# A hybrid decoder step: part tiles for split weights, down blocks behind the value tile, norms a turn earlier

## The chip, the cores and the metric

The kernel runs on one core of a Trainium2 chip. The metric is the device time of one execution in microseconds (us), less is better. TensorE (PE) does the matmuls into PSUM banks, ScalarE (ACT), VectorE (DVE) and GpSimd (POOL) do the elementwise work, and SyncE (SP) issues the DMAs. Each engine works through its instructions in the order in which they stand in its own list, and waits for others at semaphores.

## The reference

One layer of a decoder in float32, for a prompt of 2048 rows (with 16 meta rows ahead) and 8 samples of 4 rows: a mixer (an RG-LRU and a Mamba-2 part beside each other), and then a convolutional feed-forward part:

```python
def conv_ffn(h, buf, w_up, cw, cb, w_down):
    u = h @ w_up                                      # 1024 -> 2 x 3072
    u, new_buf = causal_dwconv(u, buf, cw, cb)        # 3 taps along the rows
    g, v = u[..., :D_FF], u[..., D_FF:]
    return (jax.nn.gelu(g) * v) @ w_down, new_buf     # 3072 -> 1024

def trunk(x, ...):
    ...
    h = rmsnorm(x, p['norm_mix'][l])
    m, lc, lh, sc, ss = mixer(h, ...)
    x = x + m
    h = rmsnorm(x, p['norm_ffn'][l])
    f, fc = conv_ffn(h, st_ffn_conv[l], ...)
    x = x + f
    ...
    y = rmsnorm(x, p['norm_final'])
```

Outputs are `y` for both groups of rows and the states of the scans and convolutions.

## The kernel before

**Split products.** Every float32 matrix is split into a hi part in a format that TensorE takes whole (ACT, L109) and a lo part, raw less hi (DVE, L110). A product is three matmuls: hi by hi, hi by lo, lo by hi. A weight tile has 128 x 1024 elements. It is loaded into `wraw` (or `x`, `wraw2`), and `Plain.split` writes both parts into one tile `whl`, of which there are three.

**The program list.** The phases fill a list `prog` of steps, each with the weight tiles that it uses. `build` walks through the list. Before a step it issues the loads of the tiles of the next steps (`LOADS_B` tiles ahead in the later super tiles, `AHEAD` = 2 ahead before) and then the splits that come due. The order on PE is the order of the list; on ACT, DVE and POOL a scheduler orders what the steps issue, and each queue is then served in that order.

**The mixer** takes the rows in six turns (`PLAN_A`) and ends near 960 us. It keeps its result `x` in DRAM scratch.

**The ConvFFN** takes the rows in four super tiles. The first one (S0) has the 32 sample rows and 512 rows of the prompt. For each of the 24 channel tiles kk it multiplies a gate tile (`whole_g`, PSUM bank `mm`, 48 matmuls) and a value tile (`whole_v`, bank `yy`, 48 matmuls). `conv` copies the bank into `u` (ACT, L1017 to L1020) and makes the three taps (L1101 on ACT, two times L1103 on DVE); `join` multiplies gate and value into `pm` (samples, L1042) and `p` (L1044), and splits `p` into `ph`. For the later super tiles S0 also makes four sums and differences of the half tiles of each weight pair (`Sums.add`, POOL, L955 to L958), splits them into parts `ws` (`part`), and writes the parts to DRAM scratch `wk` (`keep`).

After four channel tiles there is a block of down products in two halves (512 columns of `w_down` each), one at each of the next two kk: `m` (L1145, eight matmuls of the samples with the raw weights), then the row tiles q0 to q3 with 12 matmuls each, in two `sg` banks in turn. DVE adds each bank to `acc` (m: L1152, q: L1122). The last block stands at the end of a super tile; the sample rows are summed at L1159 and L1160. `store` normalizes and writes the result (L1138).

Later super tiles (256 + 256 columns) read the parts back and need seven products of 12 matmuls for each kk (`first_part`, `second_part`, `third_part`).

**The next super tile's rows.** `norm(q)` loads a row tile of `x`, sums its squares (ACT, L152), makes `rstd` (POOL) and multiplies (DVE, L218). `turn(p, stage)` transposes it on PE (L228) and makes the seven `h` operands on ACT, DVE and POOL (L243 to L265); stages 0 to 3 for the pair p = 0 and for the pair p = 1. `norm` of rows 0 to 2 stands at kk = 22 (after the loop in S0), `norm(3)` and the turns stand among the last down products as a `side` dictionary of positions:

```python
for z in range(4):
    side[z].append(turns[z])
    side[len(rest) - 5 + z].append(turns[4 + z])
side[3].append(lambda n=n: n.norm(3))
```

Of the kernel before, what the change touches and what calls it, by code (L numbers as in the profile page):

```python
# [17 lines left out]
P = 128  # L18
# [16 lines left out]
START = len(PLAN_A[0])  # L35
START2 = 3 * START + 1
GT_BUFS = 2
LOADS_B, SPLITS_B = 3, 3


SLOTS = {
# [32 lines left out]
def build(tc, i, o):  # L74
# [5 lines left out]
    with contextlib.ExitStack() as es:  # L80
# [31 lines left out]
        class Plain:  # L112
# [7 lines left out]
                ld(self.raw, self.src)  # L120

            def split(self, E=V):
                hl = wp.tile([P, 2, 1024], F32R, name="whl", tag="whl")
                divide(hl[:, 0], hl[:, 1], self.raw, E)
                self.out = hl[:, 0], hl[:, 1], self.raw

        def mms(ps, pairs):
            for k, (l, r) in enumerate(pairs):
# [75 lines left out]
        class Halves:  # L204
# [7 lines left out]

            def norm(self, q):
                rows, load = self.tiles[q]
                x = self.x[q] = row_tile()
                y = load(x)
                r = rstd_of(sum_squares(y[:rows], rows, D), rows, D)
                V.scalar_tensor_tensor(x[:rows], y[:rows], r[:rows], gain[:rows], op0=MUL, op1=MUL)  # L218
# [78 lines left out]
        for n, (fn, srcs) in enumerate(prog):  # L297
            if n < START:
                fn()
                continue  # L300
            if n == START2:
                begin.close()
            bound = len(flat) if n > k.begin_b else early
            b = n > k.begin_c
            while loaded < min(bound, used + len(srcs) + (LOADS_B if b else AHEAD)):
                flat[loaded].load()
                loaded += 1
            while split < min(bound, used + len(srcs) + (SPLITS_B if b else AHEAD if n >= START2 else 0)):
                flat[split].split(*(() if split else (G,)))
                split += 1  # L310
            ws = [z.out for z in flat[used:used + len(srcs)]]
            used += len(srcs)
            if fn is k.tail:
                end = es.enter_context(tc.manual_schedule(engines=order))
                continue
            fn(*ws)
# [564 lines left out]
def phase_b(k, h_b):  # L881
# [7 lines left out]
    def setup():  # L889
        k.phase.close()  # L890
        cb = k.phase.enter_context(k.tc.tile_pool(name="cb", bufs=1))
        E.sp = k.phase.enter_context(k.tc.tile_pool(name="sb", bufs=2))
        for nm, shp in (("fcw", [P, 48, 3]), ("fcb", [P, 48]), ("sel4", [P, SROWS])):
            c[nm] = cb.tile(shp, F32, name=nm, tag=nm)
            ld(c[nm], i[nm])
        c["o_fc"] = cb.tile([P, 48, 9, 2], F32, name="o_fc", tag="o_fc")
        ld(c["o_fc"][:, :, 0:NS, :], i["st_fc"])
        turn = itertools.count()
        k.raws.append(lambda: tmp("cu"[next(turn) % 2], UW, CB)[:, :512])
        k.junks.append(lambda: tmp("c", UW, CB).bitcast(BF16))  # L900

    CB, PARTS = 3, 7
# [41 lines left out]
    class Sums:  # L944


        def __init__(self, kk):
            room = {} if not kk else {"room": k.row_tile}
            self.kk = kk
            self.g = k.Plain(i["w_up"][kk], **room)  # L950
            self.v = k.Plain(i["w_up"][24 + kk], **({"room": lambda: tmp("wraw2", D, 2)} if kk else {}))

# [8 lines left out]
        def part(self, z):  # L961
            hl = E_tile("ws", 512, PARTS)
            k.divide(hl[:, 0], hl[:, 1], self.raw[z])
            if z:
                self.keep(z - 1)
            self.hl = hl

        def keep(self, z):
            ld(kept[self.kk][z], self.hl.bitcast(F32))

    S = []
    for si in range(len(PLAN_B)):
# [209 lines left out]
    def first_super_tile(t):  # L1182
        ps = [Sums(kk) for kk in range(24)]
        for kk in range(24):
            add(whole_g(t, kk), ps[kk].g)
            if kk:
                for z in range(2):
                    add(lambda z=z, p=ps[kk - 1]: p.part(z))
            if kk == 2:
                add(lambda: accs(t))  # L1190
            for b in range(NBLK - 1):
                for half in range(2):
                    if kk == NB * (b + 1) + half:
                        for fn, srcs in downs(t, b, half):
                            add(fn, *srcs)
            add(whole_v(t, kk), ps[kk].v)
            if kk:
                for z in range(2, 4):
                    add(lambda z=z, p=ps[kk - 1]: p.part(z))
            if kk:  # L1200
                add(lambda p=ps[kk - 1]: p.keep(3))
            add(ps[kk].add)

        def end():
            k.side.close()
# [1 line left out]
        add(end)  # L1207
        for z in range(4):
            add(lambda z=z: ps[23].part(z))
        add(lambda: ps[23].keep(3))  # L1210

    def later_super_tile(t):
        for kk in range(24):
# [9 lines left out]
                for fn, srcs in downs(t, *z):  # L1223
                    add(fn, *srcs)
            if kk == 22 and t is not S[-1]:
                for q in range(3):
                    add(lambda q=q: S[t.si + 1].norm.norm(q))
            add(second_part(t, kk), Value(kk), *[Kept(kk, z) for z in range(4)])

    for t in S:  # L1230
# [2 lines left out]
        (first_super_tile if t.first else later_super_tile)(t)  # L1233
        if t.first:
            k.begin_c = len(k.prog)
            for q in range(3):
                add(lambda q=q, n=n: n.norm(q))
        else:
            add(third_part(t, 23))
# [4 lines left out]
        if not last:  # L1244
            turns = [lambda p=p, s=s, n=n: n.turn(p, s) for p in range(2) for s in range(4)]
            side = {z: [] for z in range(len(rest))}
            for z in range(4):
                side[z].append(turns[z])
                side[len(rest) - 5 + z].append(turns[4 + z])
            side[3].append(lambda n=n: n.norm(3))  # L1250
        nd = len(rest) - len(rest) // (2 if t.first else 3)
        for n, (fn, srcs) in enumerate(rest):
            if n == nd:
# [113 lines left out]
```

## Time and profile before

| | |
|---|---|
| median of three runs | 2635.69 us (2634.97 to 2640.7) |
| profiled execution | 2637.97 us, span 2635.8 us, mean granted TensorE clock 0.976 |
| mixer | 0 to 960 us |
| first super tile S0 | 960 to 1476 us |
| S1, S2, S3 | to 1862, 2250 and 2636 us |
| busy: PE, DVE, ACT, POOL | 94%, 74%, 46%, 26% of the span |

Times in the profile's timelines are us from the start of the span. "Idle before" is the time in which an engine stood still ahead of an instruction, with the instruction that ended it. The names are the program's: `mm`, `yy`, `tr` and `sg` are PSUM banks, `whl` a split weight tile, `ws` a part, `h` the operands of a super tile.

### The profile page before, as it was taken

What the parts mean: (1) busy time and instruction counts of PE and PEld (TensorE: products, weight loads), DVE (VectorE), ACT (ScalarE), POOL (GpSimd) and SP (SyncE); (2) the same over time, 40 slices, a digit from 0 to 9 for tenths busy, and PEclk for the clock granted to TensorE, in tenths of its full rate; (3) what the DMA queues carried; (4) which work ended last, traced back from release to release, by engine and by line L of the source; (5) the groups of instructions that cost most, each with busy time, mean ns of one, the idle gap of its engine ahead of it and who ended that gap; (6) DMA issues with size and microseconds to landing.
All of it is one profiled execution on the core that took longest, in us unless ns stands there. A gap on an engine that the chain in (4) does not pass through costs nothing.

```text
span 2635.8 us, 42301 instructions
## 1 busy us (share of the span) xinstructions
PE 2480.6 (94%) x15834; PEld 2248.0 (85%) x15834; DVE 1948.6 (74%) x3028; ACT 1215.3 (46%) x2005; POOL 673.6 (26%) x1059
## 2 busy tenths in 40 slices
PE   7899999999989898999998999999999999999998
PEld 6578888888878787887787799998899998999997
DVE  7588878789787876666666777777777777877675
ACT  5354645456464664444445443334443334433333
POOL 4332313233232434433334300002200002200001
PEclk9899999999999999999999999999999999999999
DMA  5344252432525376454445776665776665866563
GB/s 175 105 134 134 72 177 74 155 123 79 172 81 176 101 230 239 176 207 172 164 178 215 273 264 218 234 225 192 252 252 231 218 223 179 279 238 220 208 210 129
DMA packets 153801, 486.40 MB, mean 185 GB/s; under 512 B 23334, under 2 KB 23718, under 8 KB 153596
## 3 DMA queue, kind: packets, MB, share of 16 engines
q1 hardware_dynamic: 153596, 483.70, 53.7%
q8 instruction: 125, 2.05, 0.3%
q14 instruction: 80, 0.66, 0.1%
HBM read 413.27 MB, written 70.37 MB: 183 GB/s over the span
## 4 chain that ended last, share of the span: by engine, by line
PE 67%; DVE 15%; issue 7%; POOL 4%; ACT 4%; DMA 3%; SPq 0%; DVEq 0%; POOLq 0%; ACTq 0%
PE mm L129 25%; PE sg L129 15%; PE yy L129 12%; PE tr L129 8%; DVE whl L110 3%; DVE cv L496 3%; ACT whl L109 1%; POOL wraw L956 1%; POOL wraw L955 1%; DVE acc L1122 1%; DMA wraw<-in_w_down 1%; POOL x L957 1%; PE yy L678 1%; DVE xbc L592 1%; DVE ws L110 1%
## 5 line engine op out<-in xcount | busy, mean ns | idle before, releaser
L129 PE MATMUL mm<-hhi,whl 128*128 128x384 f32 (+4 forms) x2688 | 637.9, 321 | 10.8 <-ACT xr L491 8.2
L110 DVE TENSOR_TENSOR whl<-wraw,whl 128x1024 fp32r<-128x1024 f32 x360 | 451.9, 1256 | 196.1 <-ACT whl L109 195.3
L129 PE MATMUL sg<-whl,ph 128*128 128x512 f32 x2304 | 554.6, 398 | 23.4 <-DVE acc L1122 22.8
L129 PEld LDWEIGHTS sg<-whl,ph 128*128 128x128 f32 x2304 | 431.7, 190 | 131.8 <-DVE acc L1122 30.8
L109 ACT ACTIVATE whl<-wraw 128x1024 fp32r<-128x1024 f32 x361 | 380.8, 1056 | 260.5 <-PE sg L129 105.8
L129 PEld LDWEIGHTS mm<-hhi,whl 128*128 128x128 f32 x2688 | 471.1, 193 | 17.2 <-ACT xr L491 9.9
L129 PE MATMUL mm<-hlo,whl 128*128 128x384 f32 (+4 forms) x1344 | 426.8, 318 | 0.9 <-DVE hlo L202 0.9
L1103 DVE SCALAR_TENSOR_TENSOR c<-u,fcw,c 128x512 f32<-128x512 f32 (+1 forms) x384 | 297.6, 805 | 24.6 <-ACT c L1101 20.5
L1099 POOL COPY o_fc<-u 128x2 f32<-128x2 f32 x192 | 55.5, 289 | 839.6 <-DVE u L1008 725.8
L129 PEld LDWEIGHTS mm<-hlo,whl 128*128 128x128 f32 x1344 | 259.6, 193 | 2.9 <-DVE hlo L202 1.2
L1101 ACT ACTIVATE c<-u,fcb,fcw 128x512 f32<-128x512 f32 (+1 forms) x192 | 154.0, 820 | 101.2 <-DVE u L1008 100.8
L129 PE MATMUL yy<-h,ws 128*128 128x256 f32 x1476 | 197.0, 283 | 0.0
L129 PE MATMUL tr<-h,ws 128*128 128x256 f32 x1440 | 191.9, 283 | 0.0
L129 PE MATMUL mm<-h,ws 128*128 128x256 f32 x1404 | 186.4, 282 | 4.9 <-DVE s L1069 4.9
L129 PEld LDWEIGHTS yy<-h,ws 128*128 128x128 f32 x1476 | 186.6, 190 | 1.0
L129 PEld LDWEIGHTS tr<-h,ws 128*128 128x128 f32 x1440 | 181.2, 190 | 0.7
L129 PEld LDWEIGHTS mm<-h,ws 128*128 128x128 f32 x1404 | 175.7, 189 | 5.7 <-DVE s L1069 5.3
L129 PE MATMUL mm<-whl,yhi 128*128 128x512 f32 (+1 forms) x544 | 174.7, 401 | 3.5 <-DVE whl L110 2.6
L1122 DVE TENSOR_TENSOR acc<-acc,sg 128x512 f32<-128x512 f32 x192 | 130.8, 682 | 61.3 <-PE sg L129 61.1
L129 PE MATMUL yy<-hhi,whl 128*128 128x274 f32 (+1 forms) x768 | 152.7, 292 | 4.7 <-ACT u L1020 4.7
L496 DVE SCALAR_TENSOR_TENSOR cv<-xr,packed,cv 128x384 f32<-128x384 f32 (+2 forms) x216 | 146.8, 682 | 3.4 <-ACT cv L494 0.3
L129 PEld LDWEIGHTS yy<-hhi,whl 128*128 128x128 f32 x768 | 124.8, 192 | 5.6 <-ACT u L1020 5.1
(271 smaller groups left out, 3843.7 us busy)
## 6 DMA issues: line engine op xcount, KB each, us to landing
ws<-wk SPq DMA_DIRECT2D x288, 512.0 KB, 4.8
wraw<-in_w_in SPq DMA_DIRECT2D x120, 512.0 KB, 3.6
wraw<-in_w_up SPq DMA_DIRECT2D x97, 512.0 KB, 5.1
wk<-ws SPq DMA_DIRECT2D x96, 512.0 KB, 4.6
wraw<-in_w_down SPq DMA_DIRECT2D x96, 512.0 KB, 4.1
wraw<-in_w_out SPq DMA_DIRECT2D x48, 512.0 KB, 3.6
wraw<-in_w_up SPq DMA_DIRECT2D x72, 256.0 KB, 5.4
x<-in_w_up SPq DMA_DIRECT2D x23, 512.0 KB, 6.5
```

What stands on the lines that cost most here:

```text
L109: A.activation(hi, raw, AF.Copy)
L110: E.tensor_tensor(lo, raw, hi.bitcast(F32), op=SUB)
L129: PE.matmul(ps, l, r, start=(k == 0), stop=(k == len(pairs) - 1))
L496: V.scalar_tensor_tensor(cv[:, 3:W], buf[:, t:t + NC], w[:, t:t + 1], cv[:, 3:W], op0=MUL, op1=ADD)
L592: V.scalar_tensor_tensor(xo[:, :N], th[:, 3:W], 1.0, cv[:, 3:W], op0=ADD, op1=MUL)
L678: PE.matmul(psi[:T, gsl(g)], xbc[6 + g][:, off:off + T], E.S[:, gsl(g)], start=True, stop=True)
L955: G.tensor_tensor(v1, v0, v1, op=ADD)
L956: G.tensor_tensor(v0, g0, v0, op=SUB)
L1099: G.tensor_copy(o_fc[:, g, NS, :], u[:, W - 2:W])
L1101: A.activation(cv[:, 2:W], u[:, 2:W], AF.Identity, scale=fcw[:, g, 2:3], bias=c["fcb"][:, g:g + 1])
L1103: V.scalar_tensor_tensor(cv[:, 2:W], u[:, z:z + W - 2], fcw[:, g, z:z + 1], cv[:, 2:W], op0=MUL, op1=ADD)
L1122: V.tensor_tensor(xv, xv, ps, op=ADD)
```

## The change

It has four pieces. The two parts of a weight tile become tiles of their own, `whi` and `wlo`, three of each. In S0 the step order in a channel tile is now gate, value, parts, `add`, `keep`, and then the down block if there is one; before, the block stood between gate and value. In S0 four tiles are loaded ahead (`LOADS_B1`). `norm(0)` for S1 stands at kk = 23 and the other three after the loop; later super tiles have all four norms at kk = 22, where the fourth goes to a `wraw2` tile. The turns stand at other positions of the last down products (there are 10 in S0 and 12 later).

```diff
-LOADS_B, SPLITS_B = 3, 3
+LOADS_B1, LOADS_B, SPLITS_B = 4, 3, 3
...
             def split(self, E=V):
-                hl = wp.tile([P, 2, 1024], F32R, name="whl", tag="whl")
-                divide(hl[:, 0], hl[:, 1], self.raw, E)
-                self.out = hl[:, 0], hl[:, 1], self.raw
+                hi, lo = (wp.tile([P, 1024], F32R, name=nm, tag=nm) for nm in ("whi", "wlo"))
+                divide(hi, lo, self.raw, E)
+                self.out = hi, lo, self.raw
...
-                x = self.x[q] = row_tile()
+                x = self.x[q] = k.spare_row() if q == 3 else row_tile()
...
-            while loaded < min(bound, used + len(srcs) + (LOADS_B if b else AHEAD)):
+            while loaded < min(bound, used + len(srcs) + (LOADS_B if b else LOADS_B1 if n > k.begin_b else AHEAD)):
...
+        k.spare_row = lambda: tmp("wraw2", D, 2)
...
-            if z:
-                self.keep(z - 1)
-            self.hl = hl
-
-        def keep(self, z):
-            ld(kept[self.kk][z], self.hl.bitcast(F32))
+            self.parts.append(hl)
+
+        def keep(self):
+            for z in range(4):
+                ld(kept[self.kk][z], self.parts[z].bitcast(F32))
...
+            if kk == 23:
+                add(lambda: S[1].norm.norm(0))
+            add(whole_v(t, kk), ps[kk].v)
+            if kk:
+                for z in range(2, 4):
+                    add(lambda z=z, p=ps[kk - 1]: p.part(z))
+            add(ps[kk].add)
+            if kk:
+                add(ps[kk - 1].keep)
             for b in range(NBLK - 1):
                 for half in range(2):
                     if kk == NB * (b + 1) + half:
                         for fn, srcs in downs(t, b, half):
                             add(fn, *srcs)
-            add(whole_v(t, kk), ps[kk].v)
-            if kk:
-                for z in range(2, 4):
-                    add(lambda z=z, p=ps[kk - 1]: p.part(z))
-            if kk:
-                add(lambda p=ps[kk - 1]: p.keep(3))
-            add(ps[kk].add)
...
             if kk == 22 and t is not S[-1]:
-                for q in range(3):
+                for q in range(4):
                     add(lambda q=q: S[t.si + 1].norm.norm(q))
...
-            for q in range(3):
+            for q in range(1, 4):
                 add(lambda q=q, n=n: n.norm(q))
...
-            for z in range(4):
-                side[z].append(turns[z])
-                side[len(rest) - 5 + z].append(turns[4 + z])
-            side[3].append(lambda n=n: n.norm(3))
+            for z, y in enumerate((2, 3, 4, 5, 6, 7, 8, 8) if t.first else (0, 1, 2, 3, 5, 6, 7, 8)):
+                side[y].append(turns[z])
```

On DVE in S0, from the end of a channel tile to the first additions of a down block, before (in these rows `ws` is a part, `c` a convolution, `sg` a bank of the block; line numbers after are one higher):

```order
1259 L110 TENSOR_TENSOR whl<-wraw,whl 128x1024
1260 L1103 SCALAR_TENSOR_TENSOR c<-u,fcw,c 128x560 x2
1261 L1042 TENSOR_TENSOR pm<-c 128x32
1262 L1044 TENSOR_TENSOR c<-c 128x512
1263 L110 TENSOR_TENSOR ph<-c,ph 128x512
1264 L1152 TENSOR_TENSOR acc<-acc,sg 128x512
```

The same place after:

```order
1232 L110 TENSOR_TENSOR ph<-c,ph 128x512
1233 L110 TENSOR_TENSOR wlo<-wraw,whi 128x1024
1234 L1104 SCALAR_TENSOR_TENSOR c<-u,fcw,c 128x560 x2
1235 L110 TENSOR_TENSOR wlo<-x,whi 128x1024
1236 L1104 SCALAR_TENSOR_TENSOR c<-u,fcw,c 128x560
1237 L1153 TENSOR_TENSOR acc<-acc,sg 128x512
```

The addition of m to `acc` now stands behind the gate's convolution, the lo part of the next gate tile and the first of the two taps of the value convolution; `pm` of this channel tile follows it.

On DVE at kk = 22 of S1, before, where `s` is made from a product that PE's next bank waits for:

```order
1817 L218 SCALAR_TENSOR_TENSOR x<-x,rstd,gain 128x1024
1818 L1044 TENSOR_TENSOR c<-c 128x512
1819 L218 SCALAR_TENSOR_TENSOR x<-x,rstd,gain 128x1024
1820 L110 TENSOR_TENSOR ph<-c,ph 128x512
1821 L218 SCALAR_TENSOR_TENSOR x<-x,rstd,gain 128x1024
1822 L110 TENSOR_TENSOR ws<-wraw_17947,ws 128x512
1823 L1069 TENSOR_TENSOR s_17970<-s_17852,mm 128x256
```

After:

```order
1787 L218 SCALAR_TENSOR_TENSOR x<-x,rstd,gain 128x1024
1788 L1045 TENSOR_TENSOR c<-c 128x512
1789 L218 SCALAR_TENSOR_TENSOR x<-x,rstd,gain 128x1024
1790 L110 TENSOR_TENSOR ph<-c,ph 128x512
1791 L218 SCALAR_TENSOR_TENSOR wraw_18222<-wraw_18222,rstd,gain 128x1024
1792 L1070 TENSOR_TENSOR s_18261<-s_18133,mm 128x256
```

The last of now four norms stands directly ahead of the addition to `s`; the part `ws` has moved ahead of the norms.

On DVE among the last down products of S1, before (L244 to L265 are the turns):

```order
1853 L265 TENSOR_TENSOR u<-tr,c 128x512
1854 L244 TENSOR_TENSOR h_18216<-tr,h_18216 128x4x128
1855 L218 SCALAR_TENSOR_TENSOR x<-x,rstd,gain 128x1024
1856 L244 TENSOR_TENSOR h_18215<-tr,h_18215 128x4x128
1857 L248 TENSOR_TENSOR h_18217<-u,h_18217 128x4x128
1858 L1122 TENSOR_TENSOR acc<-acc,sg 128x512 x3
```

After:

```order
1822 L265 TENSOR_TENSOR u<-tr,c 128x512
1823 L244 TENSOR_TENSOR h_18512<-tr,h_18512 128x4x128
1824 L1123 TENSOR_TENSOR acc<-acc,sg 128x512
1825 L244 TENSOR_TENSOR h_18511<-tr,h_18511 128x4x128
1826 L248 TENSOR_TENSOR h_18513<-u,h_18513 128x4x128
1827 L1123 TENSOR_TENSOR acc<-acc,sg 128x512 x2
1828 L254 TENSOR_TENSOR u<-c,tr 128x512
1829 L244 TENSOR_TENSOR h_18510<-tr,h_18510 128x4x128
```

The norm is gone from between the additions, and the second pair of turns (L254 on) begins earlier.

More of the change, by code (lines that the diff above doesn't have):

```diff
@@ L949, in __init__ @@
             self.kk = kk
+            self.parts = []
             self.g = k.Plain(i["w_up"][kk], **room)
@@ L1209, in first_super_tile @@
             add(lambda z=z: ps[23].part(z))
-        add(lambda: ps[23].keep(3))
+        add(ps[23].keep)
     def later_super_tile(t):
```

## The prediction

> **What bounds the kernel now.** I read the page first: busy shares, then the stretches of the program in a table of windows, then who waited for whom in the stretches in which TensorE (PE) idles, and last the timeline of PE at those places.
>
> ```profile
> span 2635.8 us, 42301 instructions
> PE 2480.6 (94%) x15834; PEld 2248.0 (85%) x15834; DVE 1948.6 (74%) x3028; ACT 1215.3 (46%) x2005; POOL 673.6 (26%) x1059
> L129 PE MATMUL mm<-whl,yhi 128*128 128x512 f32 (+1 forms) x544 | 174.7, 401 | 3.5 <-DVE whl L110 2.6
> L129 PE MATMUL yy<-hhi,whl 128*128 128x274 f32 (+1 forms) x768 | 152.7, 292 | 4.7 <-ACT u L1020 4.7
> ```
>
> PE is busy for 2480.6 of 2635.8 us. The change removes no matmul, so it can only shorten the 155 us in which PE idles, and the slow matmuls that follow some of these idle times.
>
> ```profile
> core 0: us, PE busy (x) PEld busy (x) DVE busy (x) ACT busy (x) POOL busy (x), PEclk, DMA share, GB/s
> 0.00:960.00 960.00, 878.17 (x4961) 776.50 (x4961) 771.56 (x1236) 508.18 (x879) 316.86 (x438) 0.96 0.41 130
> 960.00:1460.00 500.00, 455.60 (x2966) 406.74 (x2967) 330.31 (x411) 237.91 (x435) 203.74 (x253) 0.97 0.56 195
> 1500.00:1800.00 300.00, 300.00 (x2130) 282.15 (x2129) 215.63 (x359) 118.95 (x163) 27.94 (x81) 1.00 0.68 236
> 1800.00:1890.00 90.00, 81.27 (x496) 72.92 (x495) 67.16 (x102) 38.88 (x70) 24.94 (x41) 0.92 0.62 205
> 2190.00:2280.00 90.00, 81.25 (x533) 73.38 (x532) 70.26 (x108) 43.23 (x75) 25.14 (x43) 0.98 0.62 209
> ```
>
> The mixer (to 960) idles 82 us. The first ConvFFN super tile (960 to 1460) idles 44. Inside a later super tile (1500 to 1800) nothing is lost: four loads ahead or part tiles cannot gain there. At each change of super tile (1800 to 1890, 2190 to 2280) 8.7 us are lost, and in the first of these the granted clock is 0.92 as well.
>
> **The change part by part.** *Part tiles (`whi`, `wlo`).* The arithmetic, the count of matmuls and the bytes stay. PE may begin on a hi part while the lo part is made. The waits of PE for weights are small: the row of 544 matmuls above, the mixer's output projection, holds 2.6 us on DVE's lo part. The ends are a gain of 2.6 and a loss of as much, from splits that the scheduler now puts one place earlier or later among the mixer's gates; I take 0, since the order of PE there is unchanged and ACT and DVE have 452 and 188 us of idle time in that window.
>
> *Down blocks behind the value tile, first super tile.*
>
> ```profile
> PE sg L1145 <- DVE pm L1042: 18.4, 6, 9.0
> PE sg L129 <- DVE acc L1122: 16.2, 9, 2.0
> ACT ws L109 <- POOL x L957: 53.4, 23, 3.5
> ```
>
> These are the waits of the window 960 to 1460: the sample matmuls (L1145) wait for the product `pm` of the last channel tile, the down matmuls (L129) for the PSUM bank that DVE's addition to `acc` empties (there are two `sg` banks). In one period, four channel tiles with two down blocks (1109 to 1189.6), PE has these waits alone:
>
> ```profile
> PE sg L129 <- DVE acc L1122: 3.7, 2, 2.0
> PE sg L1145 <- DVE pm L1042: 1.7, 1, 1.7
> ```
>
> So a period loses 5.4 us. With the block behind the value tile, `pm` of the tile before has 48 more matmuls to become ready, and the 1.7 us go. But the block's first addition (`acc` of m) now stands on DVE behind the next gate weight's lo part and behind the first half of the value convolution, which needs PE's value product just ended. Is it late?
>
> ```profile
> 1003.37 0.28 PE L129 MATMUL mm<-hhi,whl 128*128 128x274 f32 x1
> 1009.49 0.29 PE L129 MATMUL yy<-hhi,whl 128*128 128x274 f32 x1
> 1106.84 0.38 ACT L1020 ACTIVATE u<-yy 128x272 f32<-128x272 f32 x1
> 1108.06 0.84 ACT L1101 ACTIVATE c<-u,fcb,fcw 128x560 f32<-128x560 f32 x1
> 1112.23 8.88 PE L129 MATMUL sg<-whl,ph 128*128 128x512 f32 x36
> 1159.49 0.63 ACT L109 ACTIVATE ws<-x 128x512 fp32r<-128x512 f32 x1 [3.42 <-POOL x L957]
> 1175.03 0.63 ACT L109 ACTIVATE ws<-x 128x512 fp32r<-128x512 f32 x1 [2.00 <-POOL x L957]
> ```
>
> A product of 48 matmuls takes PE 6.12 us (1003.37 to 1009.49), a channel tile 12.24. ACT's first part split comes 15.54 us after that of the tile before (1159.49 to 1175.03): the loop of value split, POOL's four additions, part splits and convolutions is 3.3 us slower than PE and catches up only while PE works on a down block. If the engines are not behind, the addition of m ends some 3.6 us after the value product (2.1 from the bank's copy to the end of L1101, 0.8 for half a convolution, 0.7 for the addition), and PE asks for that bank only after m and one q step (1.06 and 2.96, a third of 8.88), at 4.0: no wait, a gain of 5.4 a period. If they are behind by the 6.6 us of two tiles without a block, and by 3.3 after one tile, the two blocks wait 6.2 and 2.9, in sum 9.1: a loss of 3.7. The adds and part splits are now issued earlier than before (ahead of the block, not within it), which helps; the row nearest to the truth is the 15.54 against 12.24, which the change does not shorten. I take half the lag, 4.6, plus 1.3 for a lo part of the second down tile that is one split (1.2) late: 5.9, a loss of 0.5 a period. Over the five periods: +2.5, ends -27 and +18.5.
>
> In the super tile's first channel tiles there are no blocks; the value bank is late there (4.7 in two waits, the `yy` row above). The loop's excess over kk = 2 and 3 is 6.6; one more value product now comes before the first block: +0.6, between 0 and +3. The `w_down` loads lie one place further ahead in SP's queue; DMA is busy for 0.56 of the window, and PE has no DMA wait in it: 0. The `keep` DMAs, four together after the adds, move one to three places in the same queue and are waited for by nobody in this super tile: 0.
>
> *End of the first super tile.*
>
> ```profile
> 1438.06 1.92 PE L1145 MATMUL sg<-wraw,pm 128*32 128x512 f32 x2 [8.99 <-DVE pm L1042]
> 1459.65 3.60 PE L1159 MATMUL sg<-acc,sel 128*32 128x512 f32 x4 [4.21 <-DVE acc L1122]
> 1479.33 1.56 PE L129 MATMUL tr<-h,whl 128*128 128x256 f32 x11 [1.57 <-DVE h L244]
> ```
>
> The 8.99 us stays, since the last block already follows its value tile; the adds moved ahead of it give 0.8. The 4.21 us is the addition of m behind the norm of row tile 3 (L218), which is made earlier now: 0.8 is left, a gain of 3.4. The last two turns now share one place, one q step (2.96) before the next super tile, where they had two: 1.57 grows by 2. Sum -2.2, ends -5 and +3.
>
> *Changes of super tile 1 to 2 and 2 to 3.*
>
> ```profile
> 1805.28 1.28 DVE L218 SCALAR_TENSOR_TENSOR x<-x,rstd,gain 128x1024 f32<-128x1024 f32 x1 [0.44 <-POOL rstd L158]
> 1807.61 1.28 DVE L218 SCALAR_TENSOR_TENSOR x<-x,rstd,gain 128x1024 f32<-128x1024 f32 x1 [0.44 <-POOL rstd L158]
> 1808.81 0.69 DVE L110 TENSOR_TENSOR ws<-wraw,ws 128x512 fp32r<-128x512 f32 x1
> 1809.88 1.33 PE L129 MATMUL mm<-h,ws 128*128 128x256 f32 x9 [2.42 <-DVE s L1069]
> 1836.79 3.03 PE L129 MATMUL sg<-whl,ph 128*128 128x512 f32 x12 [0.91 <-DVE acc L1122]
> 1837.85 2.08 DVE L218 SCALAR_TENSOR_TENSOR x<-x,rstd,gain 128x1024 f32<-128x1024 f32 x1
> 1841.78 7.36 PE L129 MATMUL sg<-whl,ph 128*128 128x512 f32 x24 [1.96 <-DVE acc L1122]
> 1865.19 0.38 PE L129 MATMUL tr<-h,whl 128*128 128x256 f32 x1 [1.82 <-ACT h L243]
> 1867.19 2.72 PE L129 MATMUL tr<-h,whl 128*128 128x256 f32 x11 [1.62 <-DVE h L244]
> 1869.71 2.76 PE L129 MATMUL yy<-h,ws 128*128 128x256 f32 x12
> 2231.67 5.76 PE L129 MATMUL sg<-whl,ph 128*128 128x512 f32 x24 [1.98 <-DVE acc L1122]
> 2253.47 0.38 PE L129 MATMUL tr<-h,whl 128*128 128x256 f32 x1 [1.81 <-ACT h L243]
> 2255.48 2.71 PE L129 MATMUL tr<-h,whl 128*128 128x256 f32 x11 [1.62 <-DVE h L244]
> 2257.99 1.77 PE L129 MATMUL yy<-h,ws 128*128 128x256 f32 x12
> 2259.60 1.59 PE L129 MATMUL mm<-h,ws 128*128 128x256 f32 x12
> ```
>
> The norm of row tile 3 (2.08 at 1837.85) leaves the down blocks; the addition behind it (1.96, then 1.98) is on time. The last turn comes two q steps (5.9 us) earlier, so the 1.82 and 1.62, and 1.81 and 1.62, go. The slow matmuls behind them go too: 24 in 7.36 rather than 5.76, 11 in 2.72 rather than 1.46 (11/12 of 1.59), 12 in 2.76 rather than 1.59. First change: 5.40 + 1.60 + 1.26 + 1.17 = 9.4. Second: 5.41 + 1.25 + 0.18 = 6.8. The 0.91 stays. What is late next is the second product at kk = 22: a fourth norm stands ahead of L1069, 2.33 by the pitch of two of them (1805.28 to 1807.61), less the 0.60 of the `ws` part that now stands ahead of them: +1.7 each, at most 2.33 plus slow matmuls of 1.6. Net -7.7 and -5.1, sum -12.8, ends -16 and -8.
>
> The slow matmuls are priced from these rows: after nearly the same idle time the 24 took 7.36 once and 5.76 once, so they are not certain. The Trainium skill, "TensorE: Matmul & The Clock Gate", Part 1, says that the clock falls to half after an idle window of about 3.4 us and warms up again in about as long. By that rule idle times of 2 us would cost only themselves, and the two changes would give 5.40 + 5.41 - 3.4 = 7.4 instead of 12.8; the trace, with its 7.36 behind 1.96, speaks for more in one of the two.
>
> **Sum.** 0 + 2.5 + 0.6 - 2.2 - 12.8 = -11.9. From the profiled execution's 2637.97 that gives 2626.1; it stands 2.3 above the median of the runs, 2635.69, so 2623.8 against that median. 0.2% of it, 5.3 us, is about what can be told from no change.
>
> **The rivals.** *First, the first super tile gains as well.* If ACT and DVE keep up because the adds come earlier, half of the 5.4 us a period goes: -13.5 instead of +2.5, 2608. For it: ACT idles for more than half of that window. Against: the 15.54 us. Chance 0.18.
>
> *Second, slower: the addition of m is late in every block.* With the whole lag, a period waits 9.1 + 1.3 = 10.4 against 5.4: +25 over five periods in the place of +2.5, 2646. It ends measurably slower than before from the point where a period waits 5.4 + (14.4 + 5.3) / 5 = 9.3 us, the 14.4 being the other terms of the sum. For it: the two rows of ACT. Against: before, the same lag shows as waits of only 5.4. Chance 0.18.
>
> *Third, no change: the waits move.* If the fourth norm costs 2.33 and slow matmuls of 1.6 at each change, the gains at the changes are 8.4 rather than 12.8, and with the upper ends of +3 at the first super tile's end and at its start, and the +2.5, nothing measurable is left: 2636. Chance 0.17.
>
> **How the numbers follow.** The forecast, 2624, has 0.45, its own range 2614 to 2630; 0.02 is for what none of these covers. Faster: 0.45 and 0.18, less 0.02 for its edge, 0.61. Same: 0.17 and 0.03 of the forecast's and the second rival's edges, 0.20. Slower: 0.19. The range reaches to the first rival and to most of the second, 2602 to 2643: below the first by the 4 to 6 us that separate its half from the outer end of the changes, and 3 short of the second's full lag.
>
> **What the profile after would show.** Right: no wait of the sample matmuls for `pm` except at the super tile's end; at each later change no wait for `h` and no 2 us wait for `acc`, a wait of some 4 us at kk = 22. Wrong: waits of PE `sg` for `acc` of several us behind every value product, or waits for the last turn's `h` that have only moved.

## The result and the profile after

The changed kernel takes 2613.28 us (median of 4 runs, 2609.34 to 2614.27). Its ratio to the kernel before is 0.9907, with a 95% interval from 0.9887 to 0.9927: 19 to 30 us less. One further run of the kernel before, at 4379.54 us, is far slower than its other three and is not counted. The profiled execution of the changed kernel has a span of 2610.6 us.

Lines of the page of the kernel after that answer to those of before:

```profile
span 2610.6 us, 42304 instructions
PE 2466.4 (94%) x15834; PEld 2236.0 (86%) x15834; DVE 1953.0 (75%) x3028; ACT 1217.0 (47%) x2005; POOL 740.5 (28%) x1059
L129 PE MATMUL mm<-h,ws 128*128 128x256 f32 x1404 | 188.5, 284 | 9.2 <-DVE s L1070 9.2
```

The last line is the wait at kk = 22 of two super tiles, 9.2 us, taken up below. PE's busy time fell by 14.2 us with the same 15834 matmuls, and the mean granted clock rose from 0.976 to 0.983: less of the matmul time is at a lowered clock. To see where the time went, the windows of both kernels are cut at the same events: the first output projection of the mixer (its first turn), the first gate product of the ConvFFN, and the first product of the second super tile. Before:

```profile
0.00:165.81 165.81, 130.97 (x747) 111.92 (x747) 117.62 (x231) 79.12 (x169) 68.11 (x122) 0.90 0.39 129
165.81:964.68 798.87, 751.66 (x4238) 668.28 (x4238) 657.19 (x1010) 430.71 (x713) 248.75 (x317) 0.98 0.41 130
964.68:1476.07 511.39, 467.20 (x3014) 414.07 (x3013) 339.01 (x424) 245.06 (x452) 211.50 (x265) 0.97 0.55 196
1476.07:2635.80 1159.73, 1130.74 (x7841) 1053.74 (x7839) 834.75 (x1365) 460.39 (x673) 145.21 (x357) 0.99 0.65 225
```

After:

```profile
0.00:143.85 143.85, 121.59 (x747) 104.52 (x747) 116.18 (x231) 77.97 (x166) 72.48 (x122) 0.96 0.45 149
143.85:937.90 794.05, 744.54 (x4238) 661.26 (x4238) 660.00 (x1010) 433.48 (x715) 275.52 (x316) 0.99 0.42 131
937.90:1458.21 520.31, 472.20 (x3014) 418.21 (x3012) 340.53 (x421) 245.92 (x454) 246.78 (x268) 0.95 0.54 192
1458.21:2610.60 1152.39, 1128.06 (x7841) 1051.97 (x7839) 836.32 (x1368) 459.66 (x672) 145.75 (x354) 0.99 0.64 227
```

The mixer is 26.8 us shorter, 22.0 of them in its first turn. The first super tile is 8.9 us longer. The three later ones are 7.3 us shorter. So the forecast had the sum nearly right for a wrong reason: the largest piece is a term that was put at 0, and the pieces that it did price add up to 1.6 us more, not to 11.9 less.

**The mixer's first turn.** The window of 70 to 120 us before (behind the five engines' values stands PE's granted clock):

```profile
70.00:120.00 50.00, 40.99 (x175) 28.43 (x176) 26.58 (x48) 12.58 (x27) 15.40 (x29) 0.81 0.37 120
```

And after:

```profile
70.00:120.00 50.00, 48.09 (x282) 36.56 (x282) 38.47 (x67) 23.97 (x43) 29.01 (x48) 1.00 0.38 124
```

In these 50 us PE did 175 matmuls before and 282 after. The changed kernel is some way ahead in the program by then, so the two windows don't hold the same matmuls; below, the same piece of the program is compared. The waits of PE in this window before, and timelines of PE, DVE and ACT in it:

```profile
PE tr L644 <- DVE bm L641: 9.0, 3, 3.0
...
83.24 1.19 PE L644 MATMUL tr<-xdd,bm 48*128 48x256 f32 x4 [3.04 <-DVE bm L641]
84.36 1.94 PE L652 MATMUL yy<-sst,cm 128*48 128x256 f32 x4
...
76.54 1.23 DVE L110 TENSOR_TENSOR whl<-wraw,whl 128x1024 fp32r<-128x1024 f32 x1 [4.34 <-ACT whl L109]
77.69 0.55 DVE L496 SCALAR_TENSOR_TENSOR cv<-xr,packed,cv 128x328 f32<-128x328 f32 x1
...
80.90 1.33 DVE L724 SCALAR_TENSOR_TENSOR m<-th 128x328 f32<-128x328 f32 x1
82.16 0.67 DVE L656 TENSOR_TENSOR sst<-sst,tr 128x512 f32<-128x512 f32 x1
82.75 0.60 DVE L641 TENSOR_SCALAR bm<-bt,bmask 48x256 f32<-48x256 f32 x2
...
75.08 0.20 ACT L486 ACTIVATE xr<-mm 128x32 f32<-128x32 f32 x1 [4.47 <-PE mm L129]
75.45 1.06 ACT L109 ACTIVATE whl<-wraw 128x1024 fp32r<-128x1024 f32 x1
```

After:

```profile
74.26 1.13 PE L644 MATMUL tr<-xdd,bm 48*128 48x256 f32 x4 [0.37 <-DVE sst L656]
75.31 1.06 PE L652 MATMUL yy<-sst,cm 128*48 128x256 f32 x4
...
68.82 0.33 DVE L641 TENSOR_SCALAR bm<-bt,bmask 48x256 f32<-48x256 f32 x1
69.45 1.23 DVE L110 TENSOR_TENSOR wlo<-wraw,whi 128x1024 fp32r<-128x1024 f32 x1 [0.30 <-ACT whi L109]
70.88 0.35 DVE L641 TENSOR_SCALAR bm<-bt,bmask 48x256 f32<-48x256 f32 x1 [0.21 <-PE tr L644]
...
68.36 1.06 ACT L109 ACTIVATE whi<-wraw 128x1024 fp32r<-128x1024 f32 x1 [0.80 <-PE mm L129]
69.32 0.18 ACT L486 ACTIVATE xr<-mm 128x32 f32<-128x32 f32 x1
```

On ACT the split (L109) stood behind the copy of the product just ended (L486) before, and stands ahead of it now. With it the whole order of the mixer's elementwise work has shifted. Before, DVE's half of the split began at 76.54 after 4.34 us of idle time, then came five us of other work without a pause, and only behind it, at 82.75, the masked `bm` (L641) that PE waits for. Now a `bm` stands right behind the split (70.88). Three waits of PE of 3.0 us become waits of 0.4, now for DVE's addition to `sst` (L656). The four matmuls behind such a wait took 1.94 us, against 1.06.

One piece of the program, from the first L644 of a product to that of the next, has the same matmuls in both kernels. Twice in a row it took 15.46 and 16.61 us before (from 76.02, 91.48 and 108.09) and takes 11.29 and 11.28 after (from 69.71, 81.00 and 92.28). Over the first turn PE's idle time fell by 12.6 us, 7.9 of them at L644, and the time of its 747 matmuls by 9.4.

**The first super tile.** Waits of PE there after, the largest for `pm`, `acc` and weights (before: `pm` 18.4, `acc` 16.2):

```profile
PE sg L129 <- DVE acc L1153: 20.1, 8, 4.5
PE sg L1146 <- DVE pm L1043: 10.2, 1, 10.2
PE sg L129 <- DVE acc L1151: 5.0, 2, 4.5
PE sg L129 <- DVE wlo L110: 3.1, 5, 0.6
```

The wait for `pm` is gone except at the super tile's end, as was forecast. In its place stands the wait for m's addition (L1153; L1151 is the same place in the first block, where `acc` is written for the first time). Over the whole super tile PE's idle time is 48.1 us against 44.2, and its 3014 matmuls take 472.2 us against 467.2. DVE in one block after, and PE behind the wait:

```profile
1094.25 1.66 DVE L1104 SCALAR_TENSOR_TENSOR c<-u,fcw,c 128x560 f32<-128x560 f32 x2
1097.59 1.23 DVE L110 TENSOR_TENSOR wlo<-x,whi 128x1024 fp32r<-128x1024 f32 x1 [1.68 <-ACT whi L109]
1098.82 0.80 DVE L1104 SCALAR_TENSOR_TENSOR c<-u,fcw,c 128x560 f32<-128x560 f32 x1
1099.54 0.68 DVE L1153 TENSOR_TENSOR acc<-acc,sg 128x512 f32<-128x512 f32 x1
...
1100.28 0.79 PE L129 MATMUL sg<-whi,ph 128*128 128x512 f32 x1 [4.48 <-DVE acc L1153]
...
1101.29 1.05 PE L129 MATMUL sg<-whi,ph 128*128 128x512 f32 x2
```

The matmuls into m's bank ended near 1091.9; the addition waited behind the next gate tile's split, which itself waited for ACT, and behind a convolution tap. Behind the wait the granted clock was 0.50 for 6.8 us (1099.5 to 1106.3): two matmuls took 1.05 us there, and 0.62 ahead of it (at 1092.42).

### The profile page after: what moved, and what is told of

Same layout as the page of the kernel before. It is cut to its first block, busy times and chain, and to the rows that moved or that the text cites. A ratio compares the mean times of both kernels' runs of the same rounds, so it can differ in the third digit from the quotient of the medians.

```text
span 2610.6 us, 42304 instructions
## 1 busy us (share of the span) xinstructions
PE 2466.4 (94%) x15834; PEld 2236.0 (86%) x15834; DVE 1953.0 (75%) x3028; ACT 1217.0 (47%) x2005; POOL 740.5 (28%) x1059
## 4 chain that ended last, share of the span: by engine, by line
PE 58%; DVE 13%; issue 11%; POOL 8%; ACT 6%; DMA 4%; SPq 0%; POOLq 0%; DVEq 0%; ACTq 0%
PE mm L129 22%; PE sg L129 14%; PE tr L129 8%; PE yy L129 8%; DVE cv L496 3%; DVE wlo L110 2%; ACT whi L109 2%; POOL wraw L958 1%; ACT ws L109 1%; POOL wraw L957 1%; POOL o_fc L1100 1%; POOL x L959 1%; DMA wk<-ws 1%; DVE xi L741 1%; DMA x<-xo 1%
## 5 line engine op out<-in xcount | busy, mean ns | idle before, releaser
L110 DVE TENSOR_TENSOR wlo<-wraw,whi 128x1024 fp32r<-128x1024 f32 x360 | 453.9, 1262 | 155.1 <-ACT whi L109 153.6
L109 ACT ACTIVATE whi<-wraw 128x1024 fp32r<-128x1024 f32 x361 | 380.9, 1057 | 354.7 <-PE sg L129 147.6
L129 PE MATMUL sg<-whi,ph 128*128 128x512 f32 x1536 | 503.7, 401 | 30.9 <-DVE acc L1153 20.1
L129 PE MATMUL mm<-hhi,whi 128*128 128x384 f32 (+4 forms) x1344 | 432.6, 322 | 13.8 <-ACT xr L491 10.6
L129 PE MATMUL mm<-hlo,whi 128*128 128x384 f32 (+4 forms) x1344 | 424.3, 316 | 0.9 <-DVE hlo L202 0.9
L129 PE MATMUL mm<-hhi,wlo 128*128 128x384 f32 (+4 forms) x1344 | 423.4, 315 | 0.0
L129 PEld LDWEIGHTS sg<-whi,ph 128*128 128x128 f32 x1536 | 294.4, 192 | 110.7 <-DVE acc L1153 23.5
L1104 DVE SCALAR_TENSOR_TENSOR c<-u,fcw,c 128x512 f32<-128x512 f32 (+1 forms) x384 | 298.1, 791 | 22.8 <-ACT c L1102 12.6
L129 PE MATMUL sg<-wlo,ph 128*128 128x512 f32 x768 | 305.7, 398 | 3.4 <-DVE wlo L110 3.4
L129 PEld LDWEIGHTS mm<-hhi,whi 128*128 128x128 f32 x1344 | 256.6, 191 | 20.2 <-ACT xr L491 12.7
L129 PEld LDWEIGHTS mm<-hhi,wlo 128*128 128x128 f32 x1344 | 256.7, 191 | 0.0
```

The costliest lines, as they stand in the source:

```text
L109: A.activation(hi, raw, AF.Copy)
L110: E.tensor_tensor(lo, raw, hi.bitcast(F32), op=SUB)
L129: PE.matmul(ps, l, r, start=(k == 0), stop=(k == len(pairs) - 1))
L1104: V.scalar_tensor_tensor(cv[:, 2:W], u[:, z:z + W - 2], fcw[:, g, z:z + 1], cv[:, 2:W], op0=MUL, op1=ADD)
```

## The experiments

Each kernel was run in three or more rounds beside the kernel before, whose medians in these sets were 2635 to 2638 us. The three columns of stages are read from one profile of each kernel: mixer (to the first gate product), first super tile, rest. Their sum is the span of that one execution, which can lie some us beside the median.

| kernel | time, us | ratio (95% interval) | mixer | first | rest |
|---|---|---|---|---|---|
| before | 2635.7 | | 964.7 | 511.4 | 1159.7 |
| changed | 2613.3 | 0.9907 (0.9887 to 0.9927) | 937.9 | 520.3 | 1152.4 |
| parts only | 2612.95 | 0.9908 (0.9881 to 0.9935) | 945.5 | 506.8 | 1158.9 |
| no parts | 2611.95 | 0.9912 (0.9890 to 0.9934) | 959.2 | 499.0 | 1150.7 |
| downs back | 2596.68 | 0.9852 (0.9828 to 0.9876) | 939.8 | 505.5 | 1152.3 |
| hi last | 2606.62 | 0.9893 (0.9869 to 0.9918) | 958.8 | 498.8 | 1152.3 |
| hi last, first super tile | 2591.93 | 0.9836 (0.9814 to 0.9857) | 939.8 | 497.6 | 1152.1 |
| hi last, mixer | 2630.48 | 0.9975 (0.9965 to 0.9986) | 962.2 | 518.2 | 1150.9 |
| old norms | 2624.67 | 0.9955 (0.9935 to 0.9974) | 940.6 | 522.2 | 1162.3 |
| norms spread | 2584.16 | 0.9801 (0.9778 to 0.9824) | 940.4 | 498.1 | 1140.0 |
| downs back, hi last | 2605.63 | 0.9869 (0.9851 to 0.9887) | 943.5 | 510.6 | 1151.6 |
| two loads | 2591.78 | 0.9815 (0.9795 to 0.9836) | 939.4 | 498.2 | 1152.7 |
| lo block | 2564.52 | 0.9719 (0.9702 to 0.9736) | 922.3 | 499.0 | 1138.8 |
| lo block, one tile | 2638.74 | 1.0007 (0.9990 to 1.0024) | 958.9 | 515.3 | 1159.9 |

The mixer of one and the same order differs by 6 to 8 us between profiles: 958.8 to 964.7 in the five with the order of before or nearly so, 937.9 to 945.5 in the eight with the changed kernel's. The difference between the two groups lies in the first turn: 161.6 to 167.2 us in the five, 142.7 to 146.3 in the eight. Behind it the two take the same, 795.9 and 796.5 us on the average.

**Parts only.** The kernel before with this alone:

```diff
-                hl = wp.tile([P, 2, 1024], F32R, name="whl", tag="whl")
+                hi, lo = (wp.tile([P, 1024], F32R, name=nm, tag=nm) for nm in ("whi", "wlo"))
```

> The kernel before with only the split weight tile made into two tiles. Theory A (the part tiles alone give the mixer's 27 us, since they change the order of splits on ACT and DVE there; the other pieces touch only the ConvFFN): the ConvFFN starts near 938 us as in the changed kernel, the first super tile takes its 511 us of before, the rest its 1160, time near 2611. Theory B, the prediction's (part tiles give nothing, the gain lies at the changes of super tile): time near 2636, the ConvFFN starts near 965.

The mixer's gain is there with nothing else changed, 19.2 us of it, and the first super tile is 4.6 us shorter as well. In the mixer the instructions stand in the same order as in the changed kernel, on ACT, DVE, POOL and SP alike.

**No parts.** The changed kernel with the reverse of that edit.

> The changed kernel with the two parts in one tile again. Theory A: the mixer is that of before (ConvFFN from 965), the first super tile still some 520 us rather than 511, the rest 1152 rather than 1160, time near 2638. Theory B: the other pieces carry the gain, time near 2613.

The mixer lost its gain, as theory A said, but the time did not: 2612, where 2638 was expected. The first super tile, expected at 520, took 499.0. So the blocks behind the value tile do pay, and the part tiles are what spoils them. Theory A was half of it. In the changed kernel as a whole the part tiles are worth nothing: what they gain in the mixer they lose in the first super tile.

**Downs back.**

```diff
+            for b in range(NBLK - 1):
+                for half in range(2):
+                    if kk == NB * (b + 1) + half:
+                        for fn, srcs in downs(t, b, half):
+                            add(fn, *srcs)
             add(whole_v(t, kk), ps[kk].v)
...
                 add(ps[kk - 1].keep)
-            for b in range(NBLK - 1):
-                for half in range(2):
-                    if kk == NB * (b + 1) + half:
-                        for fn, srcs in downs(t, b, half):
-                            add(fn, *srcs)
```

> The changed kernel with the down blocks between gate and value again, all else as changed. Theory C (the blocks behind the value tile cost the first super tile 9 to 13 us, because the addition of m to acc stands behind the value convolution): the wait of 4.5 us for that addition goes, the first super tile takes 507 to 511 us, time near 2602. Rival (the 9 us come from the four loads ahead or the moved turns): the first super tile stays at 520, time near 2613.

505.5, just under the 507 to 511 of theory C, and a kernel 17 us faster than the changed one.

**Hi last.** What do the part tiles do to the order? In a product of 24 matmuls the last one reads the lo part; the hi tile of its own comes free one matmul earlier. If this is what puts the split ahead of the copies, then it must go when the last matmul reads the hi part:

```diff
-    for c in range(8) for z, y in ((0, 0), (0, 1), (1, 0))])
+    for c in range(8) for z, y in ((0, 0), (1, 0), (0, 1))])
```

> The changed kernel, but the last matmul of every product of 24 reads the hi part and not the lo part (hi by hi, lo by hi, hi by lo). The parts stay tiles of their own; on ACT, DVE and POOL the mixer's instructions stand again nearly as before the change (37 of the first 1000 on DVE differ, rather than 561). Theory D (the mixer's gain is the order alone: the hi tile comes free one matmul before the product ends, so the next split is placed ahead of the copies of that product): the ConvFFN starts near 965 again, time near 2638. Rival (PE gains by beginning on a hi part while the lo part is made, whatever the order): the ConvFFN starts near 938, time near 2613.

The mixer went back to 958.8, with tiles of their own and PE free to begin on a hi part: theory D. The time did not rise with it (2606.62, and 2611.63 in the profiled run that the stages are from), since the first super tile gained 21.5 by the same edit. That PE may begin on a hi part early is nothing that the part tiles brought: it did so with both parts in one tile, as in the kernel before, where a product begins behind ACT's hi part at 517.21 and its next matmul waits for DVE's lo part until 518.47.

**Hi last in the first super tile alone, and in the mixer alone.** The same line, chosen by the phase.

> The changed kernel with the lo part read last in the mixer, as changed, and the hi part read last in the first super tile's gate and value products. Theory E (one cause with two signs: the hi tile coming free one matmul before a product ends puts the next split ahead of that product's copies on ACT and DVE; this helps the mixer by 20 to 27 us and hurts the first super tile by 21): mixer to 938, first super tile 499, rest 1152, time near 2589. Rival (the two gains do not add, since the first super tile needs the late mixer's state or DMA): first super tile 510 or more, time 2600 or more.

> The reverse of the run before: the hi part is read last in the mixer's products, the lo part last in the first super tile. Theory E: mixer to 959, first super tile 520, rest 1152, time near 2631, slower than the changed kernel and within half a per cent of the kernel before. Rival (the splits' order in the first super tile does not matter, it is the time of the mixer's end that shifts both): time near 2610 as in the two runs with the mixer's old order.

Both came out as theory E said, 2592 and 2630: one cause with two signs. In the first of them DVE's order in the block is this:

```profile
1092.86 1.64 DVE L1105 SCALAR_TENSOR_TENSOR c<-u,fcw,c 128x560 f32<-128x560 f32 x2
1094.41 0.68 DVE L1154 TENSOR_TENSOR acc<-acc,sg 128x512 f32<-128x512 f32 x1
1096.46 1.23 DVE L110 TENSOR_TENSOR wlo<-x,whi 128x1024 fp32r<-128x1024 f32 x1 [1.37 <-ACT whi L109]
```

The addition of m (L1154 here) stands ahead of the next split, and PE's waits for `acc` in the super tile are small:

```profile
PE sg L129 <- DVE acc L1124: 9.0, 6, 1.7
PE sg L129 <- DVE acc L1154: 3.1, 5, 0.7
```

**Downs back with hi last.** The edit of the blocks in the kernel of the run with hi last in the first super tile.

> As the run with the hi part last in the first super tile (mixer 940, first super tile 498, rest 1152, 2592), with the down blocks between gate and value again. Theory G (the blocks behind the value tile are worth some 8 to 13 us in the first super tile once the addition of m stands ahead of the next split on DVE): first super tile 506 to 511, time 2600 to 2605. Rival (all of the first super tile's gain is the order of splits, the place of the blocks is worth nothing): 498, time near 2592.

The first super tile takes 510.6 us, as theory G had it. With the early split, it takes 505.5 with the blocks between gate and value and 520.3 with them behind; with the late split, 510.6 and 497.6. The place of the blocks is worth +15 or -13 us by where the split stands. The other kernels of the table fall into the same four groups: 505.5 to 506.8, 518.2 to 522.2, 510.6 to 515.3 (the kernel before among them) and 497.6 to 499.0.

**Two loads.**

```diff
-LOADS_B1, LOADS_B, SPLITS_B = 4, 3, 3
+LOADS_B1, LOADS_B, SPLITS_B = 2, 3, 3
```

> As the run with the hi part last in the first super tile, with two loads ahead there rather than four. By the prediction's term (no load is waited for on PE): no difference, 2590 to 2594. Rival (with the blocks behind the value tile the down weights come too late for their splits): PE waits for lo parts of the down tiles, two or more us in each of ten blocks, 2610 or more.

No difference: with the hi part read last in the first super tile, the four loads are worth nothing.

**Old norms.** The changed kernel with `norm` and `turn` at the places of before (three norms at kk = 22, the fourth and the turns in `side` as quoted above).

> The changed kernel with norms and turns at their places of before. By the prediction's term they are worth 12.8 us at the two later changes and 2.2 at the end of the first super tile: time near 2628. By the traces of the two kernels (1159.7 against 1152.4 from the second super tile on, and 4 us of one wait at the first one's end): 7 to 11 us, near 2622. Rival (the turns' moves are worth nothing, the stretch got faster through the part tiles): 2613.

The rest of the kernel takes 1162.3 us against 1152.4, and the time is 2624.67: the moves are worth some 10 us, between the two estimates.

**Norms spread.**

```diff
-            if kk == 22 and t is not S[-1]:
-                for q in range(4):
-                    add(lambda q=q: S[t.si + 1].norm.norm(q))
+            if kk in (21, 22) and t is not S[-1]:
+                for q in range(2):
+                    add(lambda q=2 * (kk - 21) + q: S[t.si + 1].norm.norm(q))
```

> As the run with the hi part last in the first super tile, and the four norms of a later super tile in two pairs, at kk = 21 and kk = 22. Theory F (the wait of 4.58 us at kk = 22 is four norms in a row ahead of one addition on DVE; two norms leave half of it): 4.58 goes to 0 to 1 at kk = 22 and something like it may stand at kk = 21; 4 to 8 us less than that run, near 2583. Rival (the pair at kk = 21 meets the down block that stands there and costs as much): no change.

DVE and PE at kk = 22 of the second super tile in the changed kernel, the last norm and the addition behind it:

```profile
1792.01 1.29 DVE L218 SCALAR_TENSOR_TENSOR wraw<-wraw,rstd,gain 128x1024 f32<-128x1024 f32 x1 [0.44 <-POOL rstd L158]
1793.21 0.42 DVE L1070 TENSOR_TENSOR s<-s,mm 128x256 f32<-128x256 f32 x1
1793.68 2.71 PE L129 MATMUL mm<-h,ws 128*128 128x256 f32 x11 [4.58 <-DVE s L1070]
```

The same product of PE in this run:

```profile
1769.97 1.69 PE L129 MATMUL mm<-h,ws 128*128 128x256 f32 x12 [0.47 <-DVE s L1071]
```

4.58 became 0.47, and 2.71 for 11 matmuls became 1.69 for 12. At two changes of super tile that is 10 of the 12 us by which the rest is shorter in these two profiles. The profiled run is the fastest of its four; by the medians the gain is 7.8 us, within theory F's 4 to 8.

**Lo block.** If the hi tile's earlier release helps the mixer, does a still earlier one help more? On the kernel with the norms spread, in the mixer alone:

```diff
-    for c in range(8) for z, y in ((0, 0), (0, 1), (1, 0))])
+    for s in (((0, 0), (0, 1)), ((1, 0),)) for c in range(8) for z, y in s])
```

> As the run with the norms in two pairs (2584), with the mixer's products in the order of 16 matmuls of the hi part and then 8 of the lo part, so that the hi tile comes free eight matmuls before the product ends rather than one. Theory E asks only that the split stands ahead of the copies, which it does already: mixer 936 to 944, time 2580 to 2588. Rival (the earlier the hi tile is free, the better): mixer 930 or less, time below 2576.

The expectation of theory E was wrong and its rival right: the mixer takes 922.3, another 18 us less. Windows of this kernel:

```profile
0.00:146.17 146.17, 120.62 (x747) 103.79 (x747) 118.53 (x230) 79.53 (x166) 70.53 (x122) 0.96 0.43 147
146.17:922.31 776.14, 744.40 (x4239) 665.50 (x4238) 654.35 (x1011) 439.17 (x715) 278.48 (x316) 0.99 0.41 134
```

The first turn is not shorter than in the changed kernel; the 18 us lie in the turns behind it. This is the fastest kernel of the study, 2564.52 us, 2.8% below the kernel before.

**Lo block, one tile.** The same order on PE in the kernel before, where every instruction of ACT, DVE, POOL and SP then stands as before.

> The kernel before, both parts in one tile, with the mixer's products in the order of 16 hi and then 8 lo matmuls. On DVE, ACT, POOL and SP every instruction stands where it stood before. Theory E (only the early release of a hi tile of its own, through the order that it makes, carries the mixer's gain): the tile comes free at the product's last matmul as before, mixer 960 to 965, time 2631 to 2641. Rival (the order on PE carries the run with the lo block: PE may begin while the lo part is made): mixer 940 or less, time below 2616.

Nothing: 1.0007. The order on PE by itself gives no time, so with tiles of their own it must work through their earlier release. Whether that is the release itself or the order that a scheduler makes of it, these two runs do not separate.

## Why the prediction was right and where its steps were wrong

The forecast was 2624 with a range of 2602 to 2643, faster at 0.61; the time is 2613.28. Range and sign hold, though the time lies just outside the forecast's own 2614 to 2630. The steps do not all hold, and that the sum came out is in part luck. From the first super tile on the forecast had 11.9 us less, and 1.6 more came; in the mixer it had nothing, and 26.8 less came. Behind this stand two effects of the part tiles that nobody priced, some 20 us less in the mixer and 21 more in the first super tile, which cancel: without part tiles the changed kernel takes 2611.95 us.

*Part tiles, put at 0 with ends of 2.6 up and down.* This is the step that failed. They are worth about 20 us in the mixer (mean of eight profiles 940.9, of five with the order of before 960.8), all of it in the first turn, and with the blocks behind the value tile they cost the first super tile 21 us (520.3 against 499.0). The 0 is right as a sum over the kernel and wrong in both its parts. Two arguments were wrong. The price was taken from what PE waits for weights by name, 2.6 us; but the gain came in waits for other things, `bm` above all, that stand behind or ahead of a split in an engine's queue. And the reordered splits were called harmless because ACT and DVE have idle time in the window; idle time on the average says nothing about what stands ahead of the one instruction that PE waits for. The changed order of the splits was seen and not followed to PE.

*Down blocks behind the value tile, +2.5 us.* The mechanism was as described, the late addition of m, and its size too: 4.48 + 0.62 in one block and 0.53 in the other make 5.6 us of waits a period, where 5.9 was forecast and 5.4 stood before. The whole lag would have made 6.2 and 2.9 in the two halves; the addition was late in one. What was left out is the price behind the wait. Three full periods took 80.65, 82.18 and 80.59 us before and 83.93, 82.98 and 82.52 after: 2.0 more on the average, of which 0.4 is waits and 1.6 is slower matmuls. From the samples' matmuls of the first half block to those of the tenth, the super tile takes 365.0 us against 351.9, 13.1 more: 6.9 in idle time, since the wait of the first block now lies within this stretch, and the rest in matmuls at a lower clock. The second cause given, the loop of 15.54 against 12.24, was not what decided: with the split one place later the same loop runs (15.45, and 15.28 in the changed kernel) and the super tile gains 13. That was the first rival's size of gain, held at 0.18; no step named the condition on which it hangs. The prediction's own sign of being wrong, waits for `acc` of several us, is there, once a period.

*Start and end of the first super tile, +0.6 and -2.2.* From the first gate product to the end of the first half block's samples it is 71.2 us against 67.7, with one product of 6.12 more in it: a gain of 2.6, about the wait for `pm` of 2.87 that stood there before. From the samples of the tenth half block on, 84.1 against 91.8 with one product less: a gain of 1.5. The wait of 4.21 went to 0.2, but the 8.99 for `pm` became 10.2, and two waits of the transposes (L228) behind the turns' `h`, 2.6 in sum, came.

*Changes of super tile, -12.8.* Measured -7.3, of which 4.7 is waits and 2.7 is faster matmuls, and -10 against the old norms in the changed kernel. The waits for `h`, 1.82 and 1.62, are gone, as forecast. The fourth norm took 4.58 - 2.42 = 2.2 us a change where 1.7 stood, and the matmuls behind it are slow (2.71 for 11), which was only in the upper end. At the first change there were slow matmuls behind the 2.42 already (the twelve from 1811.50 took 2.77), just beyond the nine that the prediction's row shows. The 1.96 for `acc` is gone from its place, but a wait of 1.69 for `acc` (at 1841.75) stands some 18 us later in the program, among the second pair's turns. No step named this one.

*Loads, 0.* Right as far as it was run: two loads do as well as four where the hi part is read last.

On the clock, the first turn shows the rule that was weighed ahead of the forecast from another side. Three idle times of 3.0 us in 40 us went with a granted clock of 0.81, and without them it was 1.00. By the piece of the program above, two of these waits cost 4.5 and 5.7 us: 15.46 less 11.29 and 16.61 less 11.28, and the 0.37 that is still waited after. The Trainium skill, "TensorE: Matmul & The Clock Gate", Part 1, puts the fall to half clock behind an idle window of about 3.4 us that runs freely. Here 3.0 us, somewhat less, was enough each time, and so were the 1.96 at 1841.78 and the 2.42 at 1809.88 before; the 1.98 and the 2.43 at the next change were not. The measured rows decide: the traces show windows of about that length, but one that is idle for little more than half is enough (see the last section).

What stays open: why the mixer's turns behind the first are 18 us shorter with the lo block. The order of all elementwise engines changes with it, and no run here takes that apart. No run holds the order and moves the release of a tile alone either; that it is the order which gives the mixer's 20 us rests on the runs in which both went together, and on the waits for `bm`. And how the scheduler weighs a tile that comes free one matmul earlier was not looked into; what is shown is that reading the hi part last takes the order back nearly to that of before, and the time with it.

## What to carry to other kernels

Where a scheduler orders the elementwise engines, a change of when a buffer comes free, even by one matmul, can reorder the whole phase; compare the orders of every phase that shares the buffer, and price the instruction that PE waits for, not the waits that carry the buffer's name. The same early release can help one phase and hurt another, so make it a choice for each phase: here the lo part last in the mixer and the hi part last in the first super tile are 21 us less than the lo part last in both and 15 less than the hi part last in both. A row of norms ahead of one small addition is spread over two steps before it is moved anywhere else.

## What the runs showed of the hardware

Waits of 3 us on PE cost more than themselves: in the first turn before, two of 3.04 and 2.98 us cost 4.5 and 5.7 us. The granted clock was 0.50 behind them, for 3.4 us (84.1 to 87.5) and for 6.8 us (97.8 to 104.6).

The length of a wait alone does not tell what follows. Before, 1.96 us at 1841.78 was followed by 24 matmuls in 7.36 us, and 1.98 at 2231.67, the same place one super tile later, by 24 in 5.76. The 2.42 at 1809.88 was followed by twelve matmuls in 2.77 us, and the 2.43 at 2201.31 by twelve in 1.63.

How the wait lies in time does tell. In all fourteen traces the granted clock changes only at steps of 3.413 us, counted through without a break, and it is 1.00 or 0.50. Cut at these steps, the traces have 10239 stretches at 1.00 whose next one is on record. All 200 in which PE was idle for more than 56% were followed by one at 0.50, none of the 9846 with less than 44% was, and of the 193 between these two shares 41 were. The four waits fit: in the stretch that held most of it, PE was idle for 1.96 and 2.0 us (57% and 59%) where the clock fell, and for 1.4 and 1.5 us (41% and 44%) where it did not, since the step cut the wait in two. So a wait of 2 or 3 us has a price of its own and, by where the step falls, a second one of 1.7 us or more: an estimate from 3.413 us at half the clock with PE busy.
